# A hybrid layer step on one core: the decoding batch's negative maximum in one operation, gating of stored tiles in raw weight buffers, and one step of the last norms left out ahead of the last weights' split

## The chip, the cores and the metric

The kernel runs on one core of one Trainium2 chip. The core has TensorE (PE) for matmuls, VectorE (DVE), ScalarE (ACT) and GpSimd (POOL) for element-wise work, and SyncE (SP), whose queue sends almost all transfers between HBM and the on-chip memory here. PEld is the loading of weights into TensorE, which runs beside the matmuls. The metric is the device time in microseconds of one execution. A profiled execution also leaves a span, from its first to its last instruction.

## The reference, cut to what matters

One layer is applied to 2048 prompt tokens and to a decoding batch of 8 sequences with 16 new tokens each, all in fp32. Group A of the heads is an mLSTM in chunks, group B is attention over a sliding window with a learned sink for each head. Then come an output projection, a layer norm, a convolutional FFN, and a second layer norm.

```
def band_attend(q, k, v, mask, sinks):
    s = einsum('bnlkgd,bnskd->bnkgls', q, k) * (A_HEAD_DIM ** -0.5)       # 64 ** -0.5 = 0.125
    ...
    mx = maximum(max(s, axis=-1), sink)
    p = exp(s - mx)
    p = p / (sum(p, axis=-1) + exp(sink - mx))
    o = einsum('bnkgls,bnskd->bnlkgd', p, v)

def conv_ffn(h, conv_prev, w_up, w_conv, b_conv, w_down):
    u = h @ w_up                                        # 1024 -> 2 x 2816
    ext = concatenate([conv_prev, u], axis=1)
    c = b_conv + sum(ext[:, j:j + T] * w_conv[j] for j in range(3))
    a, g = split(c, 2, axis=-1)
    return (silu(g) * a) @ w_down, ext[:, -2:]

def trunk_layer(...):
    ...
    h = layer_norm(alpha * x + concatenate([hm, ha]) @ w_out)
    f, conv_rows = conv_ffn(h, ...)
    y = layer_norm(alpha * h + f)
```

For the decoding batch the keys are 128 cached rows and the 16 new ones.

## The kernel before

**Tokens and products.** The 2176 tokens are 17 tiles of 128; tile 16 (`NPT`) is the decoding batch. Every fp32 operand of a dense product is split into two parts of a shorter type, hi and lo (`split`, L216: ACT casts hi in L218, DVE subtracts it in L219 to get lo), and a product is three matmuls: hi by hi, hi by lo, lo by hi. The dense products are made in blocks of tokens in a form with seven products in place of eight, so that sums and differences of quarters of the operands are formed as well.

**Order.** The order of PE's instructions is the program's (`manual_schedule`, L237). The other engines' queues, and SP's with its transfers, are ordered by the scheduler, which works from its own estimate of when each instruction can start; `high_priority` moves an instruction up, and `issue_after(x)` keeps one behind x. So an edit can also move instructions far from the edited lines.

**Stages.** From 0 to about 500 us runs the input projection (`i_dense`, matmuls of L713 and L739, evictions by ACT in L780). Three generators are woven into it by `Chains` (L158), which carries costs and due times: `t_sample` (decoding batch), `m_chain` (mLSTM) and `a_chain` (windowed attention of the prompt). They use small matmuls between the dense ones. To about 875 us runs the output projection (`o_block`), with the rest of the chains. Around 880 us `f_hT` transposes the first block's normed rows. From 890 to 1833 us runs the FFN's up-projection (`f_ups`, L1822; matmuls L1883) over three blocks of tokens (`FBLOCKS`: 6, 6 and 5 tiles): block 0 to about 1250 us, block 1 to about 1570, block 2 to 1833. A block goes over 22 channel tiles j; each has seven products of 12 matmuls, about 14.7 us. From 1833 to 2299 us runs the down-projection (`f_downs`, L2063, matmuls L2090), and until 2306.5 us the end of the last norm.

**The decoding batch's attention** (`swa_sample`, L1480 to L1543, around 220 to 290 us) handles the batch in two halves of four sequences. In each half, PE makes the scores (L1509, L1510), DVE reduces their maximum (L1511) and copies them (L1512). L1513 makes the larger of 0.125 times the maximum and the sink; L1514 subtracts it from the sink, and ACT takes the exponential (L1515); L1516 negates the maximum for use as a bias; ACT makes four exponentials with their sums (L1518). DVE adds the sink's term (L1519) and takes the reciprocal (L1520), POOL multiplies (L1521), and PE transposes the result (L1527, L1528) and multiplies it by the values. PE's queue keeps its order, so what follows the transposes there waits with them.

**The mLSTM and window chains around 300 to 340 us.** Names that the prediction uses: L860 to L863 form sums of the down-projection's weights ("txy") from loads; L1317 is the masked score of the windowed attention; L1142 weights the mLSTM's scores; L1103 is a memset of "v" on POOL; L1154 to L1176 are the head norm of the mLSTM; L1221 is the matmul "pnum"; L1307 and L1328 belong to the windowed attention.

**Up-projection, convolution and gating.** `f_evict` (L1885) empties an accumulator on ACT (L1904 and others) or DVE. `f_after` (L1923) makes the convolution of a channel tile, into a tile "cc" of 2 x 768 columns, value and gate: ACT in L1939, DVE twice in L1941. There are two "cc" buffers in the pool f3. In block 0, "cc" is stored to HBM (`zc`, L1949). In blocks 1 and 2 it is gated at once by `f_gate` (L1961: tanh on ACT in L1965, then two DVE operations, L1966 and L1967, and the store to `zf`, L1968 and L1970). Behind that, 22 times (18 in block 1, at j from 0 to 17, and 4 in block 2), a stored tile of block 0 is loaded into another "cc" buffer (L1958) and gated as well.

**Raw weights.** Weights as they come from HBM lie in a ring "wraw" of seven slots of 128 x 1024 (`WR`, L38), which all stages share. `f_raw` (L1776) loads "wv" (L1780) and "wg" for a channel tile; the split parts "uw" have ten slots. `d_weights` (L2016) loads and splits the down-projection's weights in the same ring; `self.low` is the last lo part that it made.

**The down-projection's end.** `f_downs` goes over `dseq` (block, product, unit of two channel tiles). A finished token tile is a generator in `pending`: `finish` makes its statistics, L2130 and L2132 in three steps, and `step()` takes the first two of `pending` one step further. In the last block each iteration calls `d_weights` and `d_tokens`, and then `step()` behind the last split (L2187 to L2189). L2119 and L2121 add the accumulators to "yacc"; `norm_last` (L1546 to L1554) norms the last tiles in halves and stores them.

Of the kernel before, what the change touches and what calls it, by code (L numbers as in the profile page):

```python
# [8 lines left out]
F32 = mybir.dt.float32  # L9
# [196 lines left out]
class Prog:  # L206
# [734 lines left out]
    def t_setup(self):  # L941
        nc, a, tp = self.nc, self.a, self.tp

        def ld(n):
            t = self.one("k_" + n, list(a[n].shape))
            nc.sync.dma_start(t, a[n])
            return t
        nc.sync.dma_start(self.ident, a["ident"])
        self.gb = ld("gb")
        self.mcau = ld("mcau")  # L950
        self.mswa = ld("mswa")
        self.seg = ld("seg")
        self.sink = ld("sink")
        self.sinkx = ld("sinkx")
        self.m0 = ld("m0")
        self.nsink = self.one("nsink", [P, 8])
        nc.vector.tensor_scalar_mul(self.nsink, self.sink, -1.0)
        nc.vector.tensor_scalar_mul(self.sink, self.sink, 8.0)
        self.gm = ld("gm")
        nc.vector.tensor_scalar_mul(self.gm, self.gm, 0.5)  # L960

        raw = self.work("kw", [36, MH])
        nc.sync.dma_start(raw, a["sel"])
        self.sel = self.one("sel", [36, MH], F32R)
# [12 lines left out]
        self.mc = self.M[:, P:]  # L977
        nc.vector.memset(self.mc, 0.0)
# [501 lines left out]
    def swa_sample(self, load, kvc):  # L1480
# [11 lines left out]
        mix = self.work("mixa", [P, 4, P])  # L1492
        NK = P + DS
        HB = DB // 2
        sk = self.sinkx.to_broadcast([P, HB])
        for half in range(2):
            bs = slice(half * HB, half * HB + HB)
            kc, vc = kvc
            vn = self.work("pth", [DS, HB, P], bufs=2, name="vn")
            nc.sync.dma_start(vn, self.zkv[t][half * 64:half * 64 + 64, P:].rearrange("(b l) e -> l b e", b=HB))  # L1500
            sc = self.work("sc", [P, HB, NK], bufs=2, name="scs")
            mx, es, sm = [self.work(n, [P, HB], bufs=2) for n in ("amx", "aes", "asm")]
            for b0 in (0, 2):
                ps = self.bank([P, 2, NK], "pscs")
                for i in range(2):
                    b = half * HB + b0 + i
                    for kvh in range(2):
                        rs = slice(64 * kvh, 64 * kvh + 64)
                        nc.tensor.matmul(ps[rs, i, :P], qs[rs, b], kc[rs, b0 + i], start=True, stop=True)  # L1509
                        nc.tensor.matmul(ps[rs, i, P:], qs[rs, b], ks[rs, b * DS:(b + 1) * DS], start=True, stop=True)  # L1510
                V.tensor_reduce(mx[:, b0:b0 + 2], ps, axis=AX.X, op=ALU.max)  # L1511
                V.tensor_copy(sc[:, b0:b0 + 2], ps)  # L1512
            V.scalar_tensor_tensor(mx, mx, 0.125, sk, op0=ALU.mult, op1=ALU.max)  # L1513
            V.tensor_sub(es, sk, mx)  # L1514
            nc.scalar.activation(es, es, AF.Exp)  # L1515
            V.tensor_scalar_mul(mx, mx, -1.0)  # L1516
            for b in range(HB):
                nc.scalar.activation(sc[:, b], sc[:, b], AF.Exp, bias=mx[:, b:b + 1], scale=0.125, accum_out=sm[:, b:b + 1])  # L1518
            V.tensor_add(sm, sm, es)  # L1519
            V.reciprocal(sm, sm)  # L1520
            nc.gpsimd.tensor_mul(sc, sc, sm.rearrange("p (b o) -> p b o", o=1).to_broadcast([P, HB, NK]))  # L1521
            yield 2700, 6500
            pts = self.work("pth", [P, 2, HB, P], bufs=2, name="pts")
            pp = self.bank([P, HB, P], "ppt")
            pp2 = self.bank([DS, HB, P], "ppt2")
            for i in range(HB):
                nc.tensor.transpose(pp[:, i], sc[:, i, :P], self.ident)  # L1527
                nc.tensor.transpose(pp2[:, i], sc[:, i, P:], self.ident)  # L1528
            nc.scalar.copy(pts[:, 0], pp)
            nc.scalar.copy(pts[:DS, 1], pp2)  # L1530
            yield 860, 2500

            po = self.bank([P, HB, 64], "ppo")
            for b in range(HB):
                for i, (v, p) in enumerate(((vc[:, b], pts[:, 0, b]), (vn[:, b], pts[:DS, 1, b]))):
                    for kvh in range(2):
                        cs = slice(64 * kvh, 64 * kvh + 64)
                        nc.tensor.matmul(po[cs, b], v[:, cs], p[:, cs], start=i == 0, stop=i == 1, skip_group_check=True)
            nc.scalar.copy(mix.rearrange("p j (b l) -> p j b l", b=DB)[:, :, bs], po.rearrange("p b (j l) -> p j b l", j=4))
# [383 lines left out]
    def f_after(self, b, j, s):  # L1923
# [23 lines left out]
        if b == 0:  # L1947

            nc.sync.dma_start(self.zc[j], c)  # L1949
            return  # L1950
        self.f_gate(c, b, j, WP, n)

        i = (b - 1) * NFF + j
        i = i if i < 18 else i - 6 if 24 <= i < 28 else None
        if b and i is not None:
            W0 = len(FBLOCKS[0]) * P
            c = self.f3.tile([P, 2, 768], F32, name="cc", tag="cc", bufs=2)[:, :, :W0]
            nc.sync.dma_start(c, self.zc[i])  # L1958
            self.f_gate(c, 0, i, W0, W0)

    def f_gate(self, c, b, j, WP, n):  # L1961
        nc, V = self.nc, self.nc.vector
        W = len(FBLOCKS[b]) * P
        th = self.f3.tile([P, 768], F32, name="th", tag="th", bufs=1)[:, :n]
        nc.scalar.activation(th, c[:, 1], AF.Tanh, scale=0.5)  # L1965
        V.scalar_tensor_tensor(th, th, 1.0, c[:, 1], op0=ALU.add, op1=ALU.mult)  # L1966
        V.tensor_mul(c[:, 0], th, c[:, 0])  # L1967
        nc.sync.dma_start(self.zf[b][j, :, :WP], c[:, 0, :WP])  # L1968
        if n > WP:
            nc.sync.dma_start(self.zf[b][j, :, WP:].rearrange("p (b l) -> p b l", b=DB),  # L1970
                              c[:, 0, WP:].rearrange("p (b l) -> p b l", b=DB)[:, :, 2:])

# [90 lines left out]
    def f_downs(self):  # L2063
# [73 lines left out]
        def step():  # L2137
            for f in pending[:2]:
                if next(f, self) is self:
                    pending.remove(f)  # L2140

        for g, (b, s, u) in enumerate(self.dseq):
# [41 lines left out]
                self.d_weights()  # L2184
            while self.nt < min(g + 6, len(self.dseq)):
                self.d_tokens()
            if b == nb - 1:  # L2187
                with self.tc.issue_after(self.low):
                    step()  # L2189


# [13 lines left out]
```

## Time and profile before

| | |
|---|---|
| time, median of 3 runs | 2306.07 us (2305.02 to 2309.39) |
| profiled execution, its own time | 2308.3 us |
| its span | 2306.5 us |
| mean granted TensorE clock | 0.998 |
| HBM read, written | 457.02 MB, 171.64 MB; 273 GB/s over the span |
| instructions | 39717 |

Busy time by stage, in us, with the granted clock and the mean busy share of the core's 16 DMA engines:

| stage, us | PE | DVE | ACT | POOL | clock | DMA share |
|---|---|---|---|---|---|---|
| input projection, 0 to 500 | 489.30 | 374.02 | 287.80 | 33.78 | 1.00 | 0.87 |
| output projection, 500 to 875 | 374.19 | 303.65 | 245.89 | 57.26 | 1.00 | 0.87 |
| transposes, 875 to 890 | 10.74 | 7.26 | 7.62 | 0.00 | 0.89 | 0.54 |
| up, block 0, 890 to 1250 | 359.05 | 314.96 | 211.43 | 62.39 | 1.00 | 0.78 |
| up, block 1, 1250 to 1570 | 320.00 | 233.73 | 173.38 | 37.87 | 1.00 | 0.86 |
| up, block 2, 1570 to 1833 | 261.75 | 188.97 | 141.85 | 54.86 | 1.00 | 0.89 |
| down, 1833 to 2299 | 463.02 | 381.68 | 203.43 | 26.66 | 1.00 | 0.63 |
| end, 2299 to 2306.5 | 0.00 | 4.32 | 0.00 | 0.92 | 0.69 | 0.21 |

A row of a timeline reads: start in us, length in us, engine, line of the kernel, operation, output tile <- input tiles, shape, count; in brackets the time for which the engine stood idle before it, and what is inferred to have released it. An x above 1 is a group of like instructions put into one row. A row of the table by windows has the window, its length, the busy time and count of PE, PEld, DVE, ACT and POOL, the granted clock, the DMA share and GB/s.

### The profile page before, as it was taken

The page shows a single profiled execution, that of the slowest core. Times are in us where ns is not written, and L with a number is a line of the kernel's source. Part 1 is how long each engine was busy: PE and PEld are TensorE (multiplying, and loading weights), DVE is VectorE, ACT ScalarE, POOL GpSimd, SP SyncE. Part 2 cuts the span into 40 slices and gives each one's busy share as a digit, 9 for nine tenths or more (in the row PEclk, how much of TensorE's full clock was granted, in tenths as well). Part 3 has the DMA queues.
Part 4 walks back from the last instruction along what each step waited for, and adds up shares of the span by engine and source line. Part 5 has one row for each costly group of instructions (what it writes and reads, how often), then busy time and mean ns, then how long its engine had stood idle before and what let it go on. Part 6 is the DMA issues. An engine that isn't in the chain of part 4 may idle for free. (4 is left out here: it accounts for less than half of the span.)

```text
span 2306.5 us, 39717 instructions
## 1 busy us (share of the span) xinstructions
PE 2278.0 (99%) x14293; PEld 2092.2 (91%) x14293; DVE 1808.6 (78%) x3071; ACT 1271.4 (55%) x2373; POOL 273.7 (12%) x509
## 2 busy tenths in 40 slices
PE   9999999999999999999999999999999999999998
PEld 8999999999877777999999999999999978888876
DVE  8787587777688888998778777678766786895987
ACT  5453476776766655555656555555555544444442
POOL 0001001000121110211112100013111200100100
PEclk9999999999999999999999999999999999999999
DMA  7988898899997876898778888978998786757742
GB/s 279 322 306 291 296 315 276 276 305 299 326 327 257 280 246 250 304 325 302 276 277 277 303 302 312 311 255 288 308 299 261 246 297 214 253 172 222 255 155 83
DMA packets 299733, 631.30 MB, mean 274 GB/s; under 512 B 47820, under 2 KB 141072, under 8 KB 299536
## 3 DMA queue, kind: packets, MB, share of 16 engines
q1 hardware_dynamic: 294864, 615.06, 78.2%
q0 software_dynamic: 3520, 10.56, 1.5%
q10 hardware_dynamic: 1152, 3.15, 0.4%
q8 instruction: 113, 1.85, 0.3%
q14 instruction: 84, 0.69, 0.1%
HBM read 457.02 MB, written 171.64 MB: 273 GB/s over the span
## 5 line engine op out<-in xcount | busy, mean ns | idle before, releaser
L1883 PE MATMUL fup<-hh,uw 128*128 128x384 f32 (+1 forms) x1848 | 478.2, 328 | 1.2 <-ACT ua L1904 1.2
L1883 PE MATMUL dps<-hh,uw 128*128 128x384 f32 (+1 forms) x1848 | 477.8, 328 | 0.0
L1883 PEld LDWEIGHTS fup<-hh,uw 128*128 128x128 f32 x1848 | 330.1, 188 | 1.6 <-ACT ua L1904 1.5
L1883 PEld LDWEIGHTS dps<-hh,uw 128*128 128x128 f32 x1848 | 329.9, 188 | 0.0
L1941 DVE SCALAR_TENSOR_TENSOR cc<-u,cw,cc 128x768 f32<-128x768 f32 (+1 forms) x264 | 258.1, 978 | 63.2 <-ACT cc L1939 54.8
L1883 PE MATMUL fup<-hl,uw 128*128 128x384 f32 (+1 forms) x924 | 302.6, 327 | 1.0 <-DVE hl L219 1.0
L1883 PE MATMUL dps<-hl,uw 128*128 128x384 f32 (+1 forms) x924 | 302.4, 327 | 0.0
L713 PE MATMUL dps<-w,oh 128*128 128x256 f32 x1344 | 255.5, 285 | 0.0
L218 ACT CAST uw<-wraw 128x1024 fp32r<-128x1024 f32 x126 | 123.2, 978 | 230.2 <-PE dps L2090 122.2
L219 DVE TENSOR_TENSOR w<-wraw,w 128x1024 fp32r<-128x1024 f32 (+2 forms) x163 | 186.4, 1152 | 67.6 <-ACT w L218 61.6
L713 PEld LDWEIGHTS dps<-w,oh 128*128 128x128 f32 x1344 | 211.6, 189 | 11.1 <-issue 8.1
L218 ACT CAST w<-wraw 128x1024 fp32r<-128x1024 f32 (+2 forms) x163 | 160.0, 991 | 107.1 <-PE dps L713 55.4
L219 DVE TENSOR_TENSOR uw<-wraw,uw 128x1024 fp32r<-128x1024 f32 x126 | 142.2, 1129 | 62.9 <-ACT uw L218 62.0
L713 PE MATMUL dps<-w,ol 128*128 128x256 f32 x672 | 188.3, 280 | 0.0
L2090 PE MATMUL fup<-uw,fu 128*128 128x512 f32 x726 | 173.9, 396 | 1.6 <-ACT fht L2098 1.6
L1883 PEld LDWEIGHTS fup<-hl,uw 128*128 128x128 f32 x924 | 173.5, 188 | 1.7 <-DVE hl L219 1.6
L1883 PEld LDWEIGHTS dps<-hl,uw 128*128 128x128 f32 x924 | 173.5, 188 | 0.0
L713 PE MATMUL dps<-oh,w 128*128 128x256 f32 x896 | 168.0, 282 | 3.9 <-DVE w L219 2.3
L2090 PEld LDWEIGHTS fup<-uw,fu 128*128 128x128 f32 x726 | 136.3, 188 | 34.8 <-ACT fht L2098 2.0
L2090 PE MATMUL dps<-uw,fu 128*128 128x512 f32 x660 | 165.2, 396 | 1.1 <-DVE uw L219 1.1
L1939 ACT ACTIVATE cc<-u,cw 128x768 f32<-128x768 f32 (+1 forms) x132 | 132.1, 1001 | 48.7 <-DVE u L1921 23.4
L2090 PEld LDWEIGHTS dps<-uw,fu 128*128 128x128 f32 x660 | 123.9, 188 | 31.3 <-DVE uw L219 1.5
(318 smaller groups left out, 4574.1 us busy)
## 6 DMA issues: line engine op xcount, KB each, us to landing
uw<-zw SPq DMA_DIRECT2D x176, 512.0 KB, 5.2
zw<-uw SPq DMA_DIRECT2D x88, 512.0 KB, 3.5
w<-zws SPq DMA_DIRECT2D x72, 512.0 KB, 5.8
wv<-wup SPq DMA_DIRECT2D x66, 512.0 KB, 4.7
wraw<-wi SPq DMA_DIRECT2D x65, 512.0 KB, 5.1
wraw<-zt SPq DMA_DIRECT2D x60, 512.0 KB, 4.5
wraw<-wdn SPq DMA_DIRECT2D x45, 512.0 KB, 4.4
wraw<-wo SPq DMA_DIRECT2D x40, 512.0 KB, 5.4
```

The lines of the kernel that those rows point to most:

```text
L218: nc.scalar.copy(hi, src)
L219: return nc.vector.tensor_sub(lo, src, hi.bitcast(F32)).ins
L713: mm(o, l, r, start=s in (1, 7) and c == k == i == 0, stop=k == 3 and i == 2, skip_group_check=True)
L1883: mm(ps, l[:, k], r[:, k], start=s in (1, 7) and k == 0 and i == 0, stop=k == 3 and i == 2, skip_group_check=True)
L1939: S.activation(c[:, v], u[:, 2:2 + n], AF.Identity, bias=w[3], scale=w[2])
L1941: V.scalar_tensor_tensor(c[:, v], u[:, i:i + n], w[i], c[:, v], op0=ALU.mult, op1=ALU.add)
L2090: mm(ps, l[:, k, c], r[:, k], start=s in (1, 4, 7) and u == 0 and k == 0 and i == 0, stop=u == nu - 1 and k == n - 1 and i == 2, skip_grou ...
```

## The change

Three edits in three places.

1. In `swa_sample`, a constant `nsinkx` holds the negated sink, made once in `t_setup`. L1513 now makes the smaller of -0.125 times the maximum and the negated sink, which is the negative maximum, in one operation. The sink's term is one exponential on ACT with the sink as its bias. L1514 and L1516 are gone.
2. In `f_after`, a stored tile of block 0 is loaded as two transfers of 384 KB, gate first and value second, into two tiles "cz" that are taken from the ring "wraw", where it was one transfer of 768 KB into a buffer "cc". `f_gate` takes a list of the two halves. Its arithmetic is the same.
3. In `f_downs`, the iteration of the last block in which all but one of the units' weights have been issued (`self.nw == len(self.dseq) - 1`) makes no `step()`. What is left in `pending` after the loop is carried out there.

```
@@ t_setup
+        self.nsinkx = self.one("nsinkx", [P, 1])
+        nc.vector.tensor_scalar_mul(self.nsinkx, self.sinkx, -1.0)
@@ swa_sample
-        sk = self.sinkx.to_broadcast([P, HB])
+        nsk = self.nsinkx.to_broadcast([P, HB])
...
-            V.scalar_tensor_tensor(mx, mx, 0.125, sk, op0=ALU.mult, op1=ALU.max)
-            V.tensor_sub(es, sk, mx)
-            nc.scalar.activation(es, es, AF.Exp)
-            V.tensor_scalar_mul(mx, mx, -1.0)
+            V.scalar_tensor_tensor(mx, mx, -0.125, nsk, op0=ALU.mult, op1=ALU.min)
+            nc.scalar.activation(es, mx, AF.Exp, bias=self.sinkx)
@@ f_after
-        self.f_gate(c, b, j, WP, n)
+        self.f_gate([c[:, k] for k in range(2)], b, j, WP, n)
...
-            c = self.f3.tile([P, 2, 768], F32, name="cc", tag="cc", bufs=2)[:, :, :W0]
-            nc.sync.dma_start(c, self.zc[i])
+            c = [self.wp.tile([P, 768], F32, name="cz", tag="wraw", bufs=WR)[:, :W0] for _ in range(2)]
+            for k in (1, 0):
+                nc.sync.dma_start(c[k], self.zc[i][:, k])
             self.f_gate(c, 0, i, W0, W0)
@@ f_gate
-        nc.scalar.activation(th, c[:, 1], AF.Tanh, scale=0.5)
-        V.scalar_tensor_tensor(th, th, 1.0, c[:, 1], op0=ALU.add, op1=ALU.mult)
-        V.tensor_mul(c[:, 0], th, c[:, 0])
-        nc.sync.dma_start(self.zf[b][j, :, :WP], c[:, 0, :WP])
+        nc.scalar.activation(th, c[1], AF.Tanh, scale=0.5)
+        V.scalar_tensor_tensor(th, th, 1.0, c[1], op0=ALU.add, op1=ALU.mult)
+        V.tensor_mul(c[0], th, c[0])
+        nc.sync.dma_start(self.zf[b][j, :, :WP], c[0][:, :WP])
...
@@ f_downs
-            if b == nb - 1:
+            if b == nb - 1 and self.nw != len(self.dseq) - 1:
                 with self.tc.issue_after(self.low):
                     step()
+        while pending:
+            step()
```

More of the change, by code (lines that the diff above doesn't have):

```diff
@@ L1964, in f_gate @@
         th = self.f3.tile([P, 768], F32, name="th", tag="th", bufs=1)[:, :n]
-        nc.scalar.activation(th, c[:, 1], AF.Tanh, scale=0.5)
-        V.scalar_tensor_tensor(th, th, 1.0, c[:, 1], op0=ALU.add, op1=ALU.mult)
-        V.tensor_mul(c[:, 0], th, c[:, 0])
-        nc.sync.dma_start(self.zf[b][j, :, :WP], c[:, 0, :WP])
+        nc.scalar.activation(th, c[1], AF.Tanh, scale=0.5)
+        V.scalar_tensor_tensor(th, th, 1.0, c[1], op0=ALU.add, op1=ALU.mult)
+        V.tensor_mul(c[0], th, c[0])
+        nc.sync.dma_start(self.zf[b][j, :, :WP], c[0][:, :WP])
         if n > WP:
             nc.sync.dma_start(self.zf[b][j, :, WP:].rearrange("p (b l) -> p b l", b=DB),
-                              c[:, 0, WP:].rearrange("p (b l) -> p b l", b=DB)[:, :, 2:])
+                              c[0][:, WP:].rearrange("p (b l) -> p b l", b=DB)[:, :, 2:])
     def d_begin(self):
```

## The prediction

> **What bounds the kernel.** I read the head of the page first, then the rows of TensorE (PE) that carry an idle time in brackets, then the clock by windows, and last the timelines of the other engines around each idle place.
>
> ```profile
> span 2306.5 us, 39717 instructions
> PE 2278.0 (99%) x14293; PEld 2092.2 (91%) x14293; DVE 1808.6 (78%) x3071; ACT 1271.4 (55%) x2373; POOL 273.7 (12%) x509
> ```
>
> PE is busy for 2278.0 of 2306.5 us, so 28.5 us is all that waiting costs. The change leaves PE's own instructions and their order as they are; it can only close or open waits of PE, restore the clock after one, or alter what runs after the last matmul. These are the waits near the edits (start, length, instruction, and in brackets the idle time and what is said to have ended it):
>
> ```profile
> 253.34 0.33 PE L1527 MATMUL ppt<-ident,scs 128*128 128x128 f32 x1 [2.85 <-POOL v L1103]
> 321.80 1.13 PE L1221 MATMUL pnum<-v,dt 128*128 128x129 f32 x8 [0.80 <-issue]
> 329.96 0.38 PE L713 MATMUL dps<-oh,w 128*128 128x256 f32 x1 [0.89 <-ACT mr L1163]
> 1642.59 0.41 PE L1883 MATMUL fup<-hh,uw 128*128 128x320 f32 x1 [1.25 <-ACT ua L1904]
> 2285.58 0.74 PE L2090 MATMUL dps<-uw,fu 128*128 128x512 f32 x2 [1.09 <-DVE uw L219]
> ```
>
> The windows give the granted clock (the field after the engines) around the longest of them, and around a shorter one:
>
> ```profile
> 250.00:255.00 5.00, 2.15 (x15) 1.75 (x14) 0.34 (x2) 1.91 (x9) 1.19 (x2) 0.89 0.78 280
> 255.00:260.00 5.00, 5.00 (x44) 4.57 (x42) 1.56 (x2) 2.27 (x4) 0.00 (x0) 0.77 0.79 241
> 1640.00:1645.00 5.00, 3.75 (x26) 3.49 (x25) 3.96 (x6) 2.17 (x4) 0.32 (x2) 1.00 0.79 239
> ```
>
> After the wait of 2.85 us the clock is down: (1 - 0.89) x 5 + (1 - 0.77) x 5 = 1.7 us of full speed are lost. After the wait of 1.25 us it stays at 1.00.
>
> **Edit 1, the softmax.** The chain to the wait at 253.34, first DVE, then ACT, then POOL:
>
> ```profile
> 246.67 0.15 DVE L1513 SCALAR_TENSOR_TENSOR amx<-amx,k_sinkx 128x4 f32<-128x4 f32 x1
> 248.48 0.15 DVE L1514 TENSOR_TENSOR aes<-k_sinkx,amx 128x4 f32<-128x4 f32 x1
> 248.55 1.22 DVE L219 TENSOR_TENSOR w<-wraw,w 128x1024 fp32r<-128x1024 f32 x1
> 249.69 0.16 DVE L1516 TENSOR_SCALAR amx<-amx 128x4 f32<-128x4 f32 x1
> 251.61 0.17 DVE L1519 TENSOR_TENSOR asm<-asm,aes 128x4 f32<-128x4 f32 x1 [1.77 <-ACT scs L1518]
> 247.12 0.58 ACT L780 COPY zev<-dps 128x512 f32<-128x512 f32 x1
> 248.66 0.21 ACT L1515 ACTIVATE aes<-aes 128x4 f32<-128x4 f32 x1 [0.96 <-DVE aes L1514]
> 249.88 0.41 ACT L1518 ACTIVATE scs<-scs,amx 128x144 f32<-128x144 f32 x1 [1.01 <-DVE amx L1516]
> 252.13 1.15 POOL L1521 TENSOR_TENSOR scs<-scs,asm 128x576 f32<-128x576 f32 x1 [26.37 <-DVE asm L1520]
> ```
>
> The page names the memset of L1103 as the releaser, but POOL's product L1521 ends at 253.28, just ahead of PE: that is what PE waits for. The two removed operations are only 0.15 and 0.16 us, but in DVE's queue they stand behind the large ones (L1514 1.8 us and L1516 3.0 us behind L1513). Without them the negative maximum is ready at 246.82, and ACT starts the small exponential when L780 ends, 247.70. The four large ones took from 249.88 to the sum at 251.61, 1.73 us; now they start at about 247.90 and end at 249.6. The L219 split ends at 249.77, so the sum follows at 249.70 instead of 251.61: POOL and PE come 1.9 us earlier, and PE's wait shrinks to 0.94 us. That is shorter than the 1.25 us after which the clock held, so the 1.7 us come back as well. Gain 1.9 + 1.7 = 3.6 us. Bounds: 0.3 us, the removed operations' own time, if another operation takes their place in the queue; and 2.85 + 1.7 = 4.55 if nothing is left. I take 3.6, since the new order of DVE shows the sum directly behind the split. The second half of the batch shows no wait of PE, so its shorter chain is worth nothing. The new 128x1 negation in the setup costs DVE at most one such small operation, 0.15 us, beside PE's matmuls; POOL's memset moves behind both L1521, and its reader is the matmul at 321.80.
>
> The Trainium skill, "TensorE: Matmul & The Clock Gate", section "What's actually happening", has the clock halved after an idle window of about 3.4 us. The wait here is 2.85 us and the clock fell all the same, so the row decides; by the page alone the 1.7 us would not be lost now, edit 1 would be worth 1.9 us, and the whole sum below would be 1.7 us less.
>
> **What edit 1 moves behind it.** The scheduler reorders DVE and ACT between 305 and 340 us. These rows set the waits at 321.80 and 329.96:
>
> ```profile
> 310.49 0.69 DVE L860 TENSOR_TENSOR txy<-txy 128x512 f32<-128x512 f32 x1 [1.82 <-DMA txy<-wdn]
> 313.75 0.27 DVE L1317 CUSTOM_DVE_ANT_0 sc<-psc,k_mswa 128x128 f32<-128x128 f32 x1
> 315.25 0.69 DVE L861 TENSOR_TENSOR txy<-txy 128x512 f32<-128x512 f32 x1 [0.59 <-DMA txy<-wdn]
> 321.02 0.68 DVE L1142 TENSOR_TENSOR dt<-pscore,dt 128x512 f32<-128x512 f32 x1
> 329.32 0.59 ACT L780 ACTIVATE zev<-dps 128x512 f32<-128x512 f32 x1
> ```
>
> L860 now comes after L1317, and L862 and L863 (0.69 us each) after L1142. DVE no longer stands 1.82 us for L860's load, L1317 starts 1.75 us earlier, and L1142 should end about 0.9 us earlier, which closes the 0.80 us. The eviction L780, which PE waits for at 329.96 (it ends at 329.91), stands behind an operation that waits on DVE's statistics; these come earlier now. At most 0.80 + 0.89 = 1.7 us are gained. Against that, one reciprocal (L1328) moves behind the head statistics, some 4 us later, and could open a wait of the same size as those closed, so the bounds are -1.7 and +1.7. I take a gain of 1.2, as both closed waits have a visible cause.
>
> **Edit 2, the gating.** Before, gating a stored tile took one of only two "cc" buffers. The rows of ACT ahead of the wait at 1642.59:
>
> ```profile
> 1637.35 0.85 ACT L1965 ACTIVATE th<-cc 128x768 f32<-128x768 f32 x1 [4.12 <-DMA cc<-zc]
> 1641.30 0.93 ACT L1939 ACTIVATE cc<-u,cw 128x656 f32<-128x656 f32 x1 [1.69 <-DMA zf<-cc]
> ```
>
> L1904, PE's releaser, is behind both on ACT. In the change the stored tile lies in the raw-weight ring, its loads are sent before the block's own store, and "cc" has two buffers for own tiles alone: both waits go, and the 1.25 us with them. Bounds 0 and 1.25; I take 1.25. The arithmetic is the same; one load of 768 KB becomes two of 384 KB, 22 more transfers.
>
> The price is in the ring: four allocations per channel tile instead of two, in seven slots. A new "wv" load now needs the slot of the "wg" whose split comes only three products earlier. In the steady part:
>
> ```profile
> 1411.47 0.69 DVE L219 TENSOR_TENSOR uw<-wg,uw 128x512 fp32r<-128x512 f32 x1
> 1415.81 0.62 ACT L218 CAST uw<-wv 128x512 fp32r<-128x512 f32 x1 [0.52 <-PE dps L1883]
> 1401.10 0.62 ACT L218 CAST uw<-wv 128x512 fp32r<-128x512 f32 x1 [1.13 <-PE fup L1883]
> 1413.89 1.03 ACT L1939 ACTIVATE cc<-u,cw 128x768 f32<-128x768 f32 x1 [1.31 <-DMA zf<-cc]
> DMA to landing us min/median/max: 3.7/4.8/6.6
> ```
>
> The last row is for "wv" between 1250 and 1640 us. The slot is free at 1412.16; the load lands at 1417.0 (median) or 1418.8 (slowest), 1.2 to 3.0 us after the cast at 1415.81 could start. Two casts of one kind are 14.71 us apart, seven products of 2.1 us. PE needs the weights about seven products later, so only what is behind the cast in ACT's queue counts: evictions, whose accumulator PE writes again two products later, 4.2 us. Their copies take 0.46 us (as L1904's kind), so up to 3.7 us of delay is covered, and the wait of 1.31 us at L1939 goes away. Behind the load on SP's queue stand one store, "wg", a "uw" load and the next tile's two loads; these have most of a period. Cost 0; without the cover, below.
>
> **Edit 3, the last weights.**
>
> ```profile
> 2282.45 2.47 DVE L2130 SCALAR_TENSOR_TENSOR yacc<-yacc,lmv,f_ln_g 128x1024 f32<-128x1024 f32 x2
> 2284.84 0.68 DVE L219 TENSOR_TENSOR uw<-wraw,uw 128x512 fp32r<-128x512 f32 x1
> 2293.25 0.74 DVE L1553 SCALAR_TENSOR_TENSOR yacc<-yacc,lsc,f_ln_b 128x512 f32<-128x512 f32 x1
> 2298.93 0.69 DVE L2119 SCALAR_TENSOR_TENSOR yacc<-yacc,fht 128x512 f32<-128x512 f32 x1 [1.25 <-PE fht L2090]
> ```
>
> The split goes ahead of the two L2130 and ends at 2283.1; PE asks for it at 2285.58 - 1.09 = 2284.49, so the whole 1.09 us goes, and PE ends that much earlier. DVE's work afterwards is the same, and its 1.25 us of idle time before the last L2119 shrinks to about 0.2. But in the new order one half of an L1553 (0.74 us) stands behind that L2119, ahead of the last statistics: about 0.6 us are given back. Gain 0.5; bounds 0 and 1.09.
>
> **Sum.** 3.6 + 1.2 + 1.25 + 0.5 = 6.55 us. Against the profiled execution, 2308.3 us (its span and 1.8 around it), this gives 2301.7. The median of the runs before is 2306.07, 2.2 below that execution; the forecast on its scale is 2306.07 - 6.55 = **2299.5**.
>
> **Rivals.**
> *The gain stays under what can be told.* Edit 1 moves the wait but the clock still falls (or another DVE operation fills the gap), and the reorder at 305 to 340 costs what it closes: 1.9 + 0 + 1.25 + 0.5 = 3.65, or 2302.4. For it: DVE is nearly full around 246 us, and PE still waits there. Against: the clock held after 1.25 us.
> *The ring starves (slower).* If "wv" lands more than 3.65 + 3.7 = 7.35 us after its issue, the delay passes ACT's cover and PE waits in each group. At 8 us it would be 0.65 x 18 groups = 12 us: 2306.07 + 12 - 5 = 2313. For it: the queue gets 22 more transfers. Against: the slowest "wv" of that stretch took 6.6 us.
> The Trainium skill, "DMA: Bandwidth & Descriptors", section "Measured", asks for batches of 1 MiB and more, which speaks against halving the loads and so for this rival; no run here shows yet what it costs.
> *Edit 3 gives nothing.* If the half L1553 weighs more than thought, the sum is 6.0: 2300.1, the same verdict.
>
> **How the numbers follow.** About 0.2% (4.6 us) is what a measurement of this kernel can tell from no change; faster means below 2301.5. The forecast, with its third variant, needs 4.6 of the 6.55 us: chance 0.61, own range 2297.5 to 2301.5 (all upper bounds together: 8.6 us). The small gain: 0.27. The starved ring 0.08, and a new wait at 305 to 340 larger than all gains 0.04: 0.12 slower. The range 2297.0 to 2305.5 leaves out the slower cases and little else.
>
> **What would show it.** Right: at the first ppt an idle time near 0.9 us and a clock of 1.00 after it; none at the first pnum, at the third block's fup near 1640 and at the last dps; no "DMA zf<-cc" ahead of ACT L1939; "wv" landing within 7 us. Wrong: PE rows with idle times between 1260 and 1640 us, where there are none now; the clock still below 1.00 near 250; a new wait at the first windowed attention.

## The result: 0.15% less time, a little over half of the forecast

The median of 22 runs of the changed kernel is 2303.28 us (2300.62 to 2306.79), beside 2307.08 us (2303.39 to 2310.22) for 22 runs of the kernel before. The ratio is 0.9985, with a 95% interval of 0.9979 to 0.9991: 3.5 us less, between 2.1 and 4.8. The forecast was 6.55 us less. The time lies inside the forecast range, but the gain is below the 0.2% that was set as the least that can be told from no change, so the outcome is that of the first rival, which gave 3.65 us, by its number. Its mechanism, a clock that still falls behind edit 1's wait, is not what the traces show.

The profiled execution of the changed kernel took 2302.32 us. The head of its page:

```profile
span 2300.5 us, 39831 instructions
PE 2275.4 (99%) x14293; PEld 2090.7 (91%) x14293; DVE 1811.2 (79%) x3068; ACT 1272.1 (55%) x2373; POOL 273.8 (12%) x509
```

Of the 6.0 us by which the spans of the two profiles differ, PE is busy for 2.6 us less and idle for 3.4 us less. The timeline of PE in the changed kernel, the rows with a wait at the places that the prediction named:

```profile
251.53 0.33 PE L1527 MATMUL ppt<-ident,scs 128*128 128x128 f32 x1 [0.84 <-POOL scs L1521]
318.32 1.13 PE L1223 MATMUL pnum<-v,dt 128*128 128x129 f32 x8 [0.64 <-issue]
331.95 0.33 PE L1188 MATMUL pht<-ident,hn 128*128 128x128 f32 x1 [0.53 <-ACT hn L1178]
332.72 0.33 PE L1188 MATMUL pht<-ident,hn 128*128 128x128 f32 x1 [0.44 <-ACT hn L1178]
333.54 0.62 PE L1188 MATMUL pht<-ident,hn 128*128 128x128 f32 x2 [0.48 <-ACT hn L1178]
1852.38 7.95 PE L2091 MATMUL fup<-uw,fu 128*128 128x512 f32 x33 [1.01 <-ACT fht L2099]
```

The wait at the first ppt has gone from 2.85 to 0.84 us. The waits at the first dps behind the mLSTM tile, at the third block's fup near 1640 us and at the last dps are gone. But the wait at the first pnum is still there, and three waits at the pht, 1.45 us together, stand where the kernel before had one of 0.40 us. The wait at the start of the down-projection, which the prediction did not speak of, is 1.01 us; it was 1.60 us.

The clock behind the first ppt, in the table by windows (the granted clock is the third field from the end):

```profile
250.00:255.00 5.00, 4.16 (x36) 3.88 (x36) 0.18 (x1) 2.09 (x4) 1.15 (x1) 1.00 0.99 342
255.00:260.00 5.00, 5.00 (x57) 4.33 (x57) 1.79 (x3) 1.46 (x4) 0.00 (x0) 1.00 0.60 193
```

Before, these two windows had 0.89 and 0.77. The chain to that wait, from the timelines of DVE, ACT and POOL of the changed kernel:

```profile
246.88 0.15 DVE L1515 SCALAR_TENSOR_TENSOR amx<-amx,nsinkx 128x4 f32<-128x4 f32 x1
247.80 0.30 ACT L1516 ACTIVATE aes<-amx,k_sinkx 128x4 f32<-128x4 f32 x1
248.00 0.41 ACT L1518 ACTIVATE scs<-scs,amx 128x144 f32<-128x144 f32 x1
248.69 1.22 DVE L219 TENSOR_TENSOR w<-wraw,w 128x1024 fp32r<-128x1024 f32 x1
249.82 0.15 DVE L1519 TENSOR_TENSOR asm<-asm,aes 128x4 f32<-128x4 f32 x1
250.33 1.15 POOL L1521 TENSOR_TENSOR scs<-scs,asm 128x576 f32<-128x576 f32 x1 [24.36 <-DVE asm L1520]
```

In this trace everything lies 0.10 us later than in that of the kernel before when it reaches 45 us. The exponentials start at 248.00 instead of 249.88, the sum stands right behind the split, and POOL starts 1.80 us earlier.

### The profile page after: what moved, and what is told of

It is laid out like the page before. It is cut to its first block, busy times and chain, and to the rows that moved or that the text cites. A ratio compares the mean times of both kernels' runs of the same rounds, so it can differ in the third digit from the quotient of the medians.

```text
span 2300.5 us, 39831 instructions
## 1 busy us (share of the span) xinstructions
PE 2275.4 (99%) x14293; PEld 2090.7 (91%) x14293; DVE 1811.2 (79%) x3068; ACT 1272.1 (55%) x2373; POOL 273.8 (12%) x509
## 5 line engine op out<-in xcount | busy, mean ns | idle before, releaser
L713 PEld LDWEIGHTS dps<-oh,w 128*128 128x128 f32 x896 | 139.8, 188 | 8.8 <-issue 4.1
```

Source lines behind the costliest of these rows:

```text
L713: mm(o, l, r, start=s in (1, 7) and c == k == i == 0, stop=k == 3 and i == 2, skip_group_check=True)
```

## The experiments

Each kernel's time was compared with runs of the kernel before on the same chip, made together with its own. A single run differs from the next by 2 us or so (the standard deviation of the kernel before was between 1.9 and 2.5 us in each comparison), so a kernel's gain is known to about 2 us here. The traces tell what happened in one execution of each kernel.

### Each edit alone

Edit 1 alone is the first two hunks of the diff, on the kernel before.

> Edit 1 alone. If the two profiles tell the whole truth (theory A), it is worth 1.8 us of wait, 1.7 us of clock and 0.4 us behind it: 3.9 us less than before, with a wait of about 0.84 us at the first ppt and a clock of 1.00 behind it. If the clock falls in only some executions of the kernel before (theory B), the gain of the medians is nearer 2 us. If the reordering between 300 and 340 us gives back more than the traces showed (theory C), under 1.5 us.

Measured: median 2303.75 us beside 2306.53 us, ratio 0.9987 (0.9978 to 0.9995), 3.0 us less. The wait at the first ppt is 0.84 us and the clock holds. The interval, 1.2 to 5.1 us, leaves theories A and B both standing.

Edit 2 alone is the change of `f_after` and `f_gate`.

> Edit 2 alone. Theory A: the wait of 1.25 us near 1642 us goes, and 0.6 us of the wait of 1.60 us at the start of the down-projection: 1.25 to 1.9 us less than before, and no wait of PE between 1260 and 1640 us, though ACT's casts of wv wait for their loads in some groups. The starved ring: waits of PE in the groups of the second block, and more than 2 us slower. Theory D (the gain of edit 2 varies from one execution to the next, because it hangs on when transfers land): between 0 and 1.2 us less.

Measured: median 2304.82 us, ratio 0.9993 (0.9984 to 1.0002), 1.6 us less. PE has no wait between 1260 and 1640 us. Run once more, it came out nearer to nothing:

> Edit 2 alone, once more with a trace. The theory formed from the ten traces: the stretch from 1235 to 2235 us takes 998.7 to 1002.0 us without edit 2 and 996.9 to 998.4 us with it, because waits of PE on transfers near 1642 and 1858 us become shorter and vary less. Then it takes less than 998.5 us here, without a wait near 1642, the times of the runs spread less than those of the kernel before (a standard deviation of 1 to 1.5 against 1.9 to 2.5 us), and the profiled execution lies within 1.5 us of the median. If that was chance, the stretch and the spread are those of the kernel before.

Measured: median 2305.66 us beside 2306.29 us, ratio 0.9998 (0.9989 to 1.0008). The stretch from 1235 to 2235 us took 996.85 us, as expected, and has no wait near 1642 us. But the runs spread as those of the kernel before do (standard deviation 2.2 us), so that part of the theory was chance and is dropped. In both comparisons the interval includes no change at all.

Edit 3 alone:

> Edit 3 alone. Theory A: PE's last wait of 1.09 us goes and the stretch behind the last matmul grows from 7.6 to 8.2 to 8.7 us: 0 to 0.5 us less than before, which is inside the noise. The rival that it costs time: the end grows by more than 1.1 us and the kernel is slower by up to 0.5 us.

Measured: median 2304.58 us, ratio 0.9991 (0.9981 to 1.0000). This is 2.1 us less, with an interval from 0 to 4.4 us, which does not tell the forecast 0 to 0.5 us from more. PE's last wait is gone, and the end behind the last matmul grew to 8.2 us.

The three parts add up to more (3.0 + 1.6 + 2.1 us, or 3.0 + 0.5 + 2.1) than the whole (3.5 us), but each of these is uncertain by about 2 us, so this tells nothing against their independence.

### The kernels once more, and the change without edit 1

> The kernel before, once more, with a second trace. Ratio 1.000, within 0.0006. Theory A: the second trace shows the same 2.85 us at the first ppt and a clock near 0.8 behind it, and its span is 1 to 2 us shorter than the first trace's for reasons in other places. Theory B: the wait is there but the clock holds.

Measured: median 2306.45 us, ratio 1.0000 (0.9991 to 1.0009). The second trace has the wait of 2.85 us at the first ppt, and the lowered clock behind it. Other waits on transfers differ from the first trace:

```profile
254.81 0.47 PE L1527 MATMUL ppt<-ident,scs 128*128 128x128 f32 x1 [2.85 <-POOL v L1103]
1643.02 0.41 PE L1883 MATMUL fup<-hh,uw 128*128 128x320 f32 x1 [0.80 <-ACT ua L1904]
1857.63 2.60 PE L2090 MATMUL fup<-uw,fu 128*128 128x512 f32 x10 [0.72 <-ACT fht L2098]
```

The wait near 1642 us was 1.25 us in the first trace and is 0.80 here; that at the start of the down-projection was 1.60 and is 0.72.

> The kernel before, a third trace beside it. By the same theory the stretch from 1235 to 2235 us takes more than 998.5 us, with a wait near 1642, and the profiled execution lies over 1 us above the median, as it did in the four traces of kernels without edit 2 so far (by 1.2 to 6.4 us). By chance: anything from 996.9 to 1002 us. The wait at the first ppt is 2.85 us; its clock falls in most executions.

Measured: median 2306.13 us, ratio 0.9999 (0.9991 to 1.0008). The third trace has no wait near 1642 us at all, and one of 1.99 us at the start of the down-projection; the stretch took 998.91 us. The profiled execution, 2305.86 us, lies below the median, so that expectation failed as well.

> The changed kernel once more, with a second trace. Its median lies within 1 us of 2303.3. Theory A now reads: the wait at the first ppt and its clock are the same in every execution (3.5 us of gain), while the waits on transfers differ between executions, so the first pair of profiles, 6.0 us apart, overstates the medians, 3.8 us apart. Then this trace again has a wait of 0.84 us and a clock of 1.00 at the first ppt, no wait between 1260 and 1650 us, waits of 1.4 to 1.5 us in all at the four pht near 332 us, and differs from the first trace of the changed kernel by 1 to 3 us in waits on transfers elsewhere.

Measured: median 2302.86 us beside 2305.94 us, ratio 0.9986 (0.9977 to 0.9994), the same as in the first measurement. The waits are close to what was expected: 0.84 us at the first ppt, 1.34 us at the pht, none between 1260 and 1650 us; the wait at the start of the down-projection is 0.40 us, and the one for hst near 880 us is 3.77 us.

The span of the changed kernel is 2300.5 and 2301.4 us in its two traces, and that of the kernel before 2306.5, 2306.1 and 2304.1 us in its three: the means are 4.6 us apart, not 6.0 as in the first pair.

The change without edit 1 (the softmax as before):

> The change without edit 1 (edits 2 and 3 alone). Theory A: the wait of 2.85 us and the clock near 0.83 are back at the first ppt, and it is 3 to 3.5 us slower than the changed kernel, within 1 us of the kernel before. If edits 2 and 3 carry the gain (rival), it is as fast as the changed kernel.

Measured: median 2304.35 us, ratio 0.9990 (0.9982 to 0.9999): 1.5 us slower than the changed kernel beside it, and 1.6 us faster than the kernel before, by the medians. That lies between theory A and the rival, and the noise of about 2 us does not rule out either. The wait at the first ppt is back at 2.85 us, but the clock behind it is not lowered this time. PE's timeline and the windows of this kernel:

```profile
253.68 0.33 PE L1527 MATMUL ppt<-ident,scs 128*128 128x128 f32 x1 [2.85 <-POOL v L1103]
```

```profile
252.00:254.00 2.00, 0.33 (x3) 0.31 (x4) 0.30 (x2) 0.00 (x0) 1.19 (x2) 1.00 0.94 373
254.00:256.00 2.00, 2.00 (x20) 1.94 (x18) 0.00 (x0) 1.05 (x2) 0.00 (x0) 1.00 0.47 158
```

and the same windows of the kernel before, in its first trace:

```profile
252.00:254.00 2.00, 0.67 (x6) 0.55 (x6) 0.00 (x0) 0.00 (x0) 1.19 (x2) 0.97 1.01 399
254.00:256.00 2.00, 2.00 (x11) 1.92 (x10) 0.00 (x0) 1.05 (x2) 0.00 (x0) 0.50 0.29 75
256.00:258.00 2.00, 2.00 (x14) 2.00 (x14) 0.00 (x0) 0.77 (x1) 0.00 (x0) 0.68 0.90 262
```

So the same wait costs 1.5 us of clock in one execution and nothing in another. Of eight traces with the wait of 2.85 us, seven show the lowered clock. The last section shows what decides.

### The waits behind edit 1

In the changed kernel, the head norm of the first mLSTM tile was taken ahead of two splits on DVE (`first` is true for that tile alone; the lines that hand it in are cut here):

```
-        V.scalar_tensor_tensor(r, emt, 1e18, r, op0=ALU.min, op1=ALU.max)
-        V.scalar_tensor_tensor(r, r, EPS, r, op0=ALU.mult, op1=ALU.mult)
-        V.tensor_add(r, r, mv[:, :, 1])
+        with self.tc.high_priority() if first else nullcontext():
+            V.scalar_tensor_tensor(r, emt, 1e18, r, op0=ALU.min, op1=ALU.max)
+            V.scalar_tensor_tensor(r, r, EPS, r, op0=ALU.mult, op1=ALU.mult)
+            V.tensor_add(r, r, mv[:, :, 1])
```

> The changed kernel with the three small operations of the first mLSTM tile's head norm on DVE moved ahead of two splits of 1.22 us. The theory that edit 1's reordering gained nothing because POOL's power, and ACT's scaling behind it, come no earlier: the power starts some 2.4 us earlier, the waits of 1.45 us at the four pht go, and the kernel is 1 to 1.5 us faster than the changed one, near 2302. If PE is held there by something else (the eviction or the splits that now come later), the waits only move, and the time stays at 2303.3.

Measured: median 2303.56 us, ratio 0.9995 (0.9986 to 1.0003), not faster than the changed kernel beside it (2302.86). PE's timeline:

```profile
319.05 1.13 PE L1223 MATMUL pnum<-v,dt 128*128 128x129 f32 x8 [1.02 <-issue]
336.02 0.39 PE L713 MATMUL dps<-oh,w 128*128 128x256 f32 x1 [1.72 <-ACT dps L808]
```

All waits at the pht are gone, and a single one of 1.72 us has taken their place a little later, on an eviction by ACT that is now behind the norm's work. The norm's power on POOL, in the changed kernel and then in this one:

```profile
330.41 1.05 POOL L1172 TENSOR_TENSOR ms<-mr,mhalf 128x4 f32<-128x4 f32 x1 [9.89 <-DVE mr L1171]
328.60 3.29 POOL L1172 TENSOR_TENSOR ms<-mr,mhalf 128x4 f32<-128x4 f32 x1 [7.36 <-ACT wi L1134]
```

The power did start 1.8 us earlier, but it now lay beside the two splits on DVE (328.62 to 330.97 us) and took 3.29 us in place of 1.05. So it ended at 331.89, no earlier than the 331.46 of the changed kernel, and ACT's scaling (L1178) began at 331.92 against 331.50. In the new order of ACT all four scalings, three operations of L1134 and a cast stand ahead of the eviction L808, where two scalings did, and it came at 335.39 instead of 332.57. What this run lacked was not room: between 318 and 337 us DVE is busy for 12.45 and ACT for 12.34 of 19 us.

### Halved loads without the ring

The kernel before, with the stored tile loaded in two halves into its old buffer:

```
-            nc.sync.dma_start(c, self.zc[i])
+            for k in (1, 0):
+                nc.sync.dma_start(c[:, k], self.zc[i][:, k])
```

> The kernel before, with the stored tile loaded as two transfers of 384 KB into its old cc buffer: the halving alone, without the ring. If smaller transfers cost (the rule in the Trainium skill, DMA: Bandwidth & Descriptors, section Measured), casts of wv or PE wait for loads in the second block and it is 1 to 5 us slower than before. If the halving alone brings the gain of edit 2 (the gate half is there sooner), the wait near 1642 us goes and it is up to 1 us faster. Theory A: the old buffer still sets when the load may start, the wait near 1642 us stays between 0.2 and 1.3 us, and the time is that of before.

Measured: median 2304.95 us, ratio 0.9998 (0.9988 to 1.0007): halving costs nothing that can be measured. In this trace there is no wait near 1642 us, but as the kernel before had none in its third trace either, this wait doesn't tell whether the gate half's earlier arrival helps. The whole stretch from 1235 to 2235 us, by which edit 2 is judged below, took 997.87 us here: as short as in the seven traces with edit 2 (996.85 to 998.35), and shorter than in the five with neither (998.74 to 1002.04). In this trace the stores still hold L1939 (23.3 us in 21 waits between 1250 and 1833 us). So it is open whether the ring or the halving alone shortens that stretch.

### More work on POOL, and more loads in the ring

In the changed kernel, one copy of scs onto itself ahead of L1521, in the first half of the batch only:

```
+            if half == 0:
+                nc.gpsimd.tensor_copy(sc, sc)
             nc.gpsimd.tensor_mul(sc, sc, sm...)
```

> The changed kernel with POOL's work ahead of the first half's transposes doubled: one copy of scs onto itself (about 1.1 us) before L1521, in the first half only. The wait at the first ppt grows from 0.84 to 2.0 us. So far the clock behind that wait fell in five of six traces at 2.85 us and in none of four at 0.84 us; elsewhere it fell once at 2.23 us and held once at 2.21 and at 1.89 us. Theory B now reads: the clock falls by chance, the more often the longer the wait. Then at 2.0 us it holds more often than not: 1.1 us slower than the changed kernel, about 2304.2; if it falls each time, 2.8 us slower, about 2305.8. If the first half's wait is hidden anyway (rival), 2303.1.

Measured: median 2303.16 us beside 2306.29, ratio 0.9992 (0.9983 to 1.0000). The copy took 0.69 us and began before the reciprocal was there, so the wait grew only to 1.34 us, and the clock held there; the question of a wait of 2.0 us was not put. Even this growth came through DVE:

```profile
249.77 0.69 POOL L1522 COPY scs<-scs 128x576 f32<-128x576 f32 x1 [23.79 <-ACT scs L1518]
249.83 0.65 DVE L1519 TENSOR_TENSOR asm<-asm,aes 128x4 f32<-128x4 f32 x1
```

DVE's sum, which takes 0.15 us in the changed kernel, lay beside the copy, took 0.65 us and ended with it. Of use is another row of this trace. Its timeline of PE, and its windows, at the windowed attention near 675 us:

```profile
252.04 0.33 PE L1529 MATMUL ppt<-ident,scs 128*128 128x128 f32 x1 [1.34 <-POOL scs L1523]
675.21 1.53 PE L1354 MATMUL ppt<-ident,sc 128*128 128x128 f32 x6 [1.52 <-ACT sc L1332]
```

```profile
672.00:676.00 4.00, 2.41 (x13) 1.61 (x11) 4.00 (x17) 2.17 (x6) 0.00 (x0) 1.00 0.97 347
676.00:680.00 4.00, 3.93 (x16) 3.15 (x15) 4.00 (x8) 3.18 (x9) 2.10 (x2) 0.60 1.09 358
```

Here the clock fell behind a wait of 1.52 us. It also fell at 335.48 us, behind the three waits at the pht, none of which is longer than 0.53 us.

The rival of the starved ring was provoked by sending each wv load of the second and third block twice:

```
-        nc.sync.dma_start(v, self.a["wup"][j])
+        for _ in range(2 if b else 1):
+            nc.sync.dma_start(v, self.a["wup"][j])
```

> The changed kernel with each wv load of the second and third block sent twice (512 KB more ahead of each wg load, 22.5 MB in all): the ring's starved rival, provoked. A wv load then lands some 1.8 us later at about 300 GB/s. In the changed kernel ACT's casts of wv wait up to 2.7 us for their load, and PE does not wait. If some 3.7 us of delay are covered, as the prediction had it, casts wait up to 4.5 us and PE waits in a few groups alone: 1 to 5 us slower than the changed kernel. If the cover is used up already, each of some 40 groups loses 1 to 1.8 us: 40 us or more. If the cover is larger, or the transfers have room, the time stays within 1 us.

Measured: median 2307.71 us, ratio 1.0007 (0.9998 to 1.0016). Beside the changed kernel's ratios, 0.9985 and 0.9986, this is some 5 us slower, at the upper end of the first case. What its tile "wv" waited for between 1250 and 1640 us, and PE's waits in its timeline:

```profile
  DMA wv<-wup: 35.9, 20
```

```profile
1744.49 0.42 PE L1884 MATMUL fup<-hh,uw 128*128 128x320 f32 x1 [2.48 <-ACT ua L1905]
1833.47 0.42 PE L1884 MATMUL dps<-hh,uw 128*128 128x320 f32 x1 [0.72 <-ACT ub L1913]
```

ACT's casts waited 35.9 us for their loads, in 20 places, 3.6 us at the longest, and PE had no wait in that time. In the third block, where a product is shorter, a cast waited 4.23 us (at 1668.14) and PE only 0.16 us behind it; behind one that waited 7.58 us (at 1741.24), PE waited the 2.48 us shown, for an eviction that stood behind that cast on ACT. So the cover that the prediction counted on, 3.7 us, is real, and it has an end. In this trace the clock fell also at 319.96 us, behind the wait of 1.39 us at the first pnum.

## Why the prediction came out as it did

The traces allow each term to be measured by itself, as the time from the start of one matmul to that of another, which PE's rows give in every kernel (for the end, from the last matmul's end to the span's end). All in us:

| stretch, and the edit that acts in it | without the edit (traces) | with it (traces) | difference | forecast |
|---|---|---|---|---|
| wait at L780's release, 45 us, to first ppt; edit 1 | 208.41 (8) | 206.50 (5) | -1.91 | -1.9 |
| first ppt to the wait at the first pnum; edit 1, clock | 67.66 (7 of 8), 66.14 (1) | 66.12 (4) | -1.5 in 7 of 8 | -1.7 |
| from there to the pcol behind the pht; edit 1, order | 17.94 (8) | 18.06 (3) | +0.1 | -1.2 |
| second block's first wait to 2235 us; edit 2 | 999.87 (5) | 997.64 (7) | -2.2 | -1.25 |
| 2235 us to the last matmul's end; edit 3 | 63.37 (7) | 62.00 (7) | -1.37 | -1.09 |
| last matmul's end to the span's end; edit 3 | 7.7 (7) | 8.5 (7) | +0.8 | +0.6 |

Left out of "with it" are the kernel with more POOL work in the first row, those with more POOL work or loads in the second, these and the one with the norm moved in the third, and the one with more loads in the fourth; the halved loads are left out of the fourth row's "without". Their values are 207.01 in the first row; 66.16 and 66.59 in the second; 18.69, 18.58 and 18.90 in the third, in the first two of which the clock fell; and 1003.16 (more loads) and 997.87 (halved loads) in the fourth.

**Edit 1's wait: right.** The predicted start of the exponentials (247.90) and end of the sum (249.7 to 249.9) came out as 248.00 and 249.97, and the stretch to it shrank by the 1.9 us that were worked out from the queue, not by the 0.3 us of the removed operations.

**Edit 1's clock: right in kind, too sure in size.** A wait of 0.84 us held the clock in all five traces. But the 1.7 us of the kernel before are not lost in each execution: in seven traces of eight, 1.5 us. As a mean that is 1.3 us. The Trainium skill, "TensorE: Matmul & The Clock Gate", section "What's actually happening", says that the activity is judged in windows of about 3.4 us that run freely, without regard to the kernel. The traces agree in this: the clock changes on a grid of 3.41 us (last section), and a cell of it, the time from one of its points to the next, loses 1.7 us at half the clock. They do not agree that it takes an idle time as long as the window: 2.07 us of idle time in one cell always sufficed, and 1.46 us did once.

**The reorder at 305 to 340 us: the step that failed.** The prediction gave 1.2 us for two waits closed "as both have a visible cause". One, at the first pnum, was not closed; it is 0.64 to 1.03 us in the changed kernel's two traces, and 0.21 to 1.89 us in the eight without edit 1. The prediction had it that DVE "no longer stands 1.82 us for L860's load". In the changed kernel it stands longer for it, only later:

```profile
311.97 0.69 DVE L860 TENSOR_TENSOR txy<-txy 128x512 f32<-128x512 f32 x1 [2.40 <-DMA txy<-wdn]
317.54 0.69 DVE L1144 TENSOR_TENSOR dt<-pscore,dt 128x512 f32<-128x512 f32 x1
```

L1144 (L1142 before) makes what pnum reads. In all six traces with edit 1 DVE waits 2.4 to 3.6 us for that load, and pnum starts 6.4 to 6.6 us behind L860. Counted from the first ppt, L1144 came 1.67 us earlier than in the first trace of the kernel before, but PE came 1.5 us earlier too, as its clock was not lowered.

The other wait was closed and came back at the pht. Without the wait at pnum, the third row's stretch is 17.1 us in each of the eight traces and 17.1 to 17.2 us in the three, though the wait of 0.9 to 1.0 us at the dps is gone from these. These rows show it; DVE and ACT of the kernel before:

```profile
333.50 0.16 DVE L1169 TENSOR_TENSOR mr<-mr,bmv 128x4 f32<-128x4 f32 x1
334.89 0.69 ACT L1176 ACTIVATE hn<-hn,ms 128x128 f32<-128x128 f32 x2 [2.74 <-POOL ms L1170]
```

and of the changed kernel:

```profile
330.11 0.15 DVE L1171 TENSOR_TENSOR mr<-mr,bmv 128x4 f32<-128x4 f32 x1
331.50 0.40 ACT L1178 ACTIVATE hn<-hn,ms 128x128 f32<-128x128 f32 x1 [1.91 <-POOL ms L1172]
```

Both moved by 3.39 us, no more than everything else had moved already. PE, which no longer stopped for 0.89 us at the dps, arrived at the pht that much before they were ready. The prediction asked what closes a wait and not what is late next, and that part of the first rival by which this stretch "costs what it closes" is what happened.

**Edit 2: right in sign, sized from one execution.** The 1.25 us near 1642 us do go; but in five traces without edit 2 that wait was 1.25, 0.80, 0, 0.25 and 0.84 us (the last in two parts), 0.6 in the mean, and the prediction took the largest for the rule. More came from a place that it had not looked at: the wait at the start of the down-projection is 1.60, 0.72, 1.99, 2.21 and 2.23 us in those five traces, and 0 to 1.46 us, 0.7 in the mean, in the seven with edit 2. In one, edit 1 alone, the clock fell behind it as well, which makes the longest stretch, 1002.04 us. Why the loads of the gated rows come earlier there was not followed. As the trace with halved loads alone is as short, and the timed runs give 1.6 and 0.5 us for edit 2 with intervals that include 0, the 2.2 us are not shown to be the ring's.

The ring's price was as forecast. The changed kernel's tile "wv" between 1250 and 1640 us, and two rows of ACT:

```profile
  DMA wv<-wup: 12.1, 6
...
DMA to landing us min/median/max: 4.3/5.5/6.7
```

```profile
1612.36 0.62 ACT L218 CAST uw<-wv 128x512 fp32r<-128x512 f32 x1 [2.59 <-DMA wv<-wup]
1624.76 0.94 ACT L1939 ACTIVATE cc<-u,cw 128x656 f32<-128x656 f32 x1 [2.69 <-POOL u L1937]
```

The loads land within 7 us, six casts wait for theirs, and PE for none; later, at 1663.31, a cast waits 3.97 us, and PE does not stop there either. The store no longer holds L1939. The rule on batches in "DMA: Bandwidth & Descriptors" (the Trainium skill, section "Measured") did not come to bear: halved loads alone gave a ratio of 0.9998.

**Edit 3: right.** PE's 1.09 us go (the stretch is 1.37 us shorter; the rest was not followed), and 0.8 us are given back at the end. The last rows of DVE in the changed kernel:

```profile
2276.75 0.68 DVE L219 TENSOR_TENSOR uw<-wraw,uw 128x512 fp32r<-128x512 f32 x1
2291.85 0.69 DVE L2120 SCALAR_TENSOR_TENSOR yacc<-yacc,fht 128x512 f32<-128x512 f32 x1 [0.58 <-PE fht L2091]
2292.45 0.74 DVE L1553 SCALAR_TENSOR_TENSOR yacc<-yacc,lsc,f_ln_b 128x512 f32<-128x512 f32 x1
2295.47 1.41 DVE L1553 SCALAR_TENSOR_TENSOR yacc<-yacc,lsc,f_ln_b 128x512 f32<-128x512 f32 x2
```

The half of L1553 stands behind the last accumulation, as the order told. DVE's idle time ahead of that accumulation shrank from 1.25 to 0.58 us, not to the forecast 0.2: it is DVE that sets this end, and only the idle time that is taken from it is won.

**The sum.** By these means the terms give 1.9 + 1.3 - 0.1 + 2.2 + 0.6 = 5.9 us, against 3.5 us (2.1 to 4.8) in the timed runs. The rest is not settled. From the pcol behind the pht to the first matmul of the up-projection, where no edit acts, the changed kernel's two traces take 563.8 and 565.2 us, and the eight without edit 1 563.0 to 566.4 us, with 564.1 in the mean: waits on transfers, and the clock behind the wait of 2.2 to 3.8 us near 880 us, come out differently each time. All six traces with edit 1 have a mean of 565.4 us. That would be 1.3 us paid back, but it is not clear of this spread. So that the time came out at the first rival's number, and inside a range of 8.5 us, is in part luck: the clock, which that rival had falling, was restored.

## What to carry to other kernels

A wait that hangs on a transfer, or a lowered clock behind a wait, differs from one execution to the next; one trace shows one draw, and a term read from it wants a second trace. Where a wait of the engine that sets the time is closed, ask what that engine reaches next, and whether that came earlier by more than the shift itself; if not, the gain is paid back there. A small operation between large ones in a queue costs its place, not its length: removing 0.31 us of DVE work won 1.9 us.

## What the runs showed of the hardware

**The clock behind a wait.** Taken by the length of the wait, it looks like chance. The clock fell to 0.50 behind 2.85 us in seven traces of eight, behind 2.23 us (edit 1 alone), 1.52 us (more POOL work) and 1.39 us (doubled loads), and held behind 2.93 us near 882 us (edit 2 alone), 2.48 us (doubled loads), 2.21 us (edit 3 alone) and 1.99 us (the third trace of the kernel before). Near 880 us, where PE waits for transfers of hst, both ends of this are seen. With edit 2 alone the clock is 1.00 behind a wait of 2.93 us that ended at 882.79; with edit 3 alone it is 0.50 until 890.46 us, behind one of 2.47 us that ended at 884.84. The shorter wait was followed by over 5 us at half the clock, the longer one by none.

What decides is where the wait lies on a grid of 3.41 us. In each trace the clock falls at points that are whole multiples of 3.4133 us apart (in the first trace of the kernel before at 253.86, 881.91 and 2301.86 us: 184 and 416 steps), and until the last matmul it stays at 0.50 for one, two or three steps. The grid lies differently in each execution. Windows cut along it show the same wait of 2.85 us, first in the kernel before, in a single cell (a cell is the time from one point of the grid to the next), then without edit 1, split over two:

```profile
250.45:253.86 3.41, 0.56 (x6) 0.49 (x6) 0.34 (x2) 1.13 (x6) 1.19 (x2) 1.00 0.88 320
253.86:257.27 3.41, 3.41 (x19) 3.26 (x18) 0.00 (x0) 1.09 (x3) 0.00 (x0) 0.50 0.56 164
```

```profile
249.02:252.44 3.42, 1.81 (x16) 1.60 (x14) 1.51 (x4) 1.89 (x9) 0.00 (x0) 1.00 0.75 243
252.44:255.85 3.41, 2.17 (x19) 2.10 (x20) 0.00 (x0) 1.05 (x2) 1.19 (x2) 1.00 0.70 269
```

PE (the first of the busy times) is idle for 2.85 us of the cell in the first case, and the next cell has 0.50; in the second it is idle for 1.61 and 1.24 us, and the clock holds. Between 20 and 2290 us of the fourteen traces, the clock fell behind each of the 18 cells in which PE was idle for 2.07 us or more, behind 5 of the 15 with 1.46 to 1.84 us, and behind none with less; what decides between 1.46 and 1.84 us is open. (In the first 10 us, which are left out, it fell in four traces behind cells with 1.20 to 1.73 us.) By this count a single wait of 0.84 us is too short to lower the clock, and one of 2.85 us escapes only where neither of its parts is over 1.84 us, an estimate of a quarter of the grid's positions ((1.84 - 1.01) / 3.41); it escaped once in eight.

**POOL and DVE beside each other.** The power of the head norm (L1170) runs 17 times in the kernel before: nine times it takes 1.03 to 1.05 us, eight times 1.4 to 2.5 us. Each of these eight lies beside operations of DVE, as the one of 3.29 us with the norm moved does, and as DVE's sum of 0.65 us lay beside a copy on POOL. Three of the nine short ones lie beside operations of DVE too, so not every such neighbour costs time; which do was not tested.

**The delay that ACT absorbed.** Casts of weights waited up to 3.97 us for their loads in the changed kernel, and up to 3.6 us between 1250 and 1640 us with doubled loads, and PE did not stop for them; behind a cast that waited 7.58 us it did.
